# Rotations, score sums and convolution taps of a token mixer: running values in PSUM banks instead of SBUF tiles

## The chip, the cores and the metric

One core of a Trainium2 chip runs the whole program in one launch. The metric is the device time of that launch in microseconds (us); the kernel before takes 1549.39 us as the median of three runs (1548.85 to 1549.53). Engines carry the names of the profile: PE is TensorE (matmuls), PEld its weight loads, DVE is VectorE, ACT is ScalarE, POOL is GpSimd, SP the sync engine, which issues most loads.

## The reference

Two layers of a decoder trunk over 512 tokens of width 1024, all in float32. Each layer is a token mixer, a residual LayerNorm, a feed-forward block with a short convolution and a second residual LayerNorm. The mixer is the part that the change touches:

```python
z = h @ w_in + b_in
u_pool, u_conv, q, k, v, qi, ki, wi, gates = split_cols(z, IN_SIZES)
q, k = rope(q), rope(k)                       # 8 query heads, 2 key heads of 64
qi, ki = rope(qi) * 64**-0.5, rope(ki)        # indexer: 8 heads of 64, one key
y_pool = pool_mixer(u_pool) @ w_pool_out      # windows 2, 4, 8, 16
y_conv = conformer_conv(u_conv) @ w_conv_out  # GLU, causal conv of 31 taps, LayerNorm, swish
score = sum_h wi[h] * relu(qi[h] . ki)        # causal
y_attn = attention over the 128 best keys of each query @ w_attn_out
h = layer_norm(alpha * h + (sum_i sigmoid(gate_i) * y_i) @ w_o)
```

`rope(x)` is `x * cos + swap_halves(x) * sin` with signs in the sine table.

## The kernel before

Activations stand transposed, channels on partitions and the 512 tokens along the free axis. Matrix products keep float32 accuracy by splitting each operand into a high and a low part and summing three products, so every weight chunk of 128x1024 is loaded by SP, rounded by ACT (L74, `w_hi`) and subtracted by DVE (L78, `w_lo`; some chunks on POOL, in two halves). There are 123 chunks per layer, 246 in all; `Weights.take` hands them out in the order in which they are used, and four pairs of split tiles are in flight.

The eight PSUM banks are dealt out by tag: three `a`, two `s`, two `p`, one `v` (`BANKS`). A tile of a tag waits for a bank of that tag whose last reader is done. Before the change a projection's bank is read by ACT into an SBUF tile (`t`, with the bias) and is free again.

`mix` runs once per layer. It starts with the projections of the indexer's key (`head.os[0]`), the attention's key (`head.os[1]`) and the first pooling tile, which the preceding block has prepared (`Head`). Then come the four tiles of the indexer's queries (two heads each), the pooling, gate and value tiles of the convolution, v, and the four tiles of the attention's queries. `rotate` turns a tile: four DMAs on ACT's queue swap the halves into a second tile (`sw`), POOL multiplies that by the sine table (L409), DVE multiplies the tile by the cosine table (L408) and adds the two (L410). `stack` rounds a rotated tile on ACT (L417) and subtracts on DVE (`split_lo`, L112).

Three kinds of work are generators, and the main line steps them between projections. `index_gen(i)`, for query blocks 1 to 3, computes for each of eight heads a product (bank `s`), a relu on ACT into a tile `u` (three of them), and a multiply-add on DVE into `sc`, the block's score (L475 for the first head, L477 for the others); it then finds the 128 best keys by 16 pairs of L484 and L485 and turns the score into a mask. `conv_gen` runs the 31 taps of the two halves of the convolution's channels: for each half seven taps on DVE (L592, L595), 23 by a scaling on ACT (L589, tile `cvt`, two of them) and an addition on POOL (L590), and the sum of both at L598. `attn_gen(i)` is the attention of a block. After q come eight gates of the pooling branch: a projection, a small projection `y`, and DVE's L729, which multiplies them and frees the bank of `y`; then further gates, the branch merge (L748, L762, L766) and the output projection.

The order on each engine isn't that of the code. The tile framework plans it from a timeline of its own and writes a fixed list per engine; each engine takes its list from front to back and waits at the first instruction whose inputs aren't there.

Of the kernel before, what the change touches and what calls it, by code (L numbers as in the profile page):

```python
# [11 lines left out]
AF = mybir.ActivationFunctionType  # L12
ALU = mybir.AluOpType
PSUM = bass.MemoryType.PSUM

P = 128
D = 1024
L = 512
# [71 lines left out]
def trunk_kernel(ctx, tc, x, positions, w, poolw, params, lnv, cons, out):  # L90
# [264 lines left out]
    def mix(l, head, prev, ln, nxt):  # L355
        es = ExitStack()
        with es:
# [8 lines left out]
            def t_slot(dt=F32):  # L366
                return slot("t", 4, dt)
# [33 lines left out]
            def rotate(t, c0, slot_a, slot_s):  # L401
# [5 lines left out]
                a = slot_a()  # L407
                V.tensor_tensor(out=a[:, 0:n], in0=t[:, 0:n], in1=cosT[:, c0:L], op=ALU.mult)  # L408
                G.tensor_tensor(out=sw[:, 0:n], in0=sw[:, 0:n], in1=sinT[:, c0:L], op=ALU.mult)  # L409
                V.tensor_tensor(out=a[:, 0:n], in0=a[:, 0:n], in1=sw[:, 0:n], op=ALU.add)  # L410
                return a[:, 0:n]
# [16 lines left out]
            a = rotate(t, 0, p_slot, p_slot)  # L428
# [10 lines left out]
            t = t_slot()  # L439
            A.activation(t, head.os[1], AF.Identity, bias=pb(1))  # L440
            a = rotate(t, 0, p_slot, p_slot)
# [11 lines left out]
            for j in range(4):  # L453
                o = in_tile(P)
                t = t_slot()
                A.activation(t[:, 0:L - P], o[:, 0:L - P], AF.Identity, bias=pb(2 + j))
                tag = "qa" if j < 2 else "qb"
                qi.append(stack(rotate(t, P, p_slot, p_slot), q_slot(tag)[:, 0:L - P], q_slot(tag)[:, 0:L - P]))
# [3 lines left out]
            def index_gen(i):  # L462
                wd = (i + 1) * P
                sc = slot(f"mask{i}", 1, F32, [P, wd])
                for hh in range(NH):
# [8 lines left out]
                    if hh == 0:  # L474
                        V.tensor_scalar(sc, rl[:, 0:wd], wc, None, op0=ALU.mult)  # L475
                    else:
                        V.scalar_tensor_tensor(out=sc, in0=rl[:, 0:wd], scalar=wc, in1=sc,  # L477
                                               op0=ALU.mult, op1=ALU.add)
# [95 lines left out]
            def conv_gen():  # L574
                accs = []
                for c in range(2):
                    acc, pacc = c_slot()[:, 0:L], c_slot()[:, 0:L]
# [20 lines left out]
                    V.tensor_tensor(out=acc, in0=acc, in1=pacc, op=ALU.add)  # L598
                    accs.append(acc)
# [59 lines left out]
            for j in range(4):  # L659
                o = in_tile()  # L660
                t = t_slot()
                A.activation(t, o, AF.Identity, bias=pb(13 + j))
                stack(rotate(t, 0, t_slot, t_slot), qa_hi[:, j, :], qa_lo[:, j, :])
                step(1.5, 8)
# [252 lines left out]
```

## Time and profile before

| what | value |
|---|---|
| median of three runs | 1549.39 us (1548.85 to 1549.53) |
| profiled execution, its own time | 1548.56 us |
| its span, first to last instruction | 1546.8 us |
| mean granted TensorE clock | 0.983 of the upper level |
| PE busy | 1467.5 us, 95% of the span |
| DVE busy | 1007.5 us, 65% |
| ACT busy | 683.6 us, 44% |
| POOL busy | 538.1 us, 35% |

The shares are means over stages that are limited by different engines. The first mix begins at about 40 us and the second at about 798 us; the feed-forward blocks take up the rest. The table of stages gives each engine's busy time in a stretch, the granted clock and the DMA share; the list by form gives for each kind of instruction its count, busy time, mean duration in ns and the idle time in front of it.

### The profile page before, as it was taken

The numbers are of one execution on the slowest core, as the hardware profiler recorded it, in microseconds if no ns is written. First come the engines' busy times: TensorE is split into PE (matmuls) and PEld (weight loads), VectorE is DVE, ScalarE is ACT, GpSimd is POOL, SyncE is SP. The second block draws the span as 40 slices with busy tenths as digits, with TensorE's granted clock in tenths as the row PEclk, the third lists the DMA queues.
The fourth block names the chain that finished last, engine by engine and source line by source line (L and its number), as shares of the span: only waits on it lengthen the run. The fifth ranks groups of instructions, "written<-read, shape, count | busy, mean of one in ns | idle before, by whom it ended". The sixth has DMA issues, their size and how long they took to land.

```text
span 1546.8 us, 18617 instructions
## 1 busy us (share of the span) xinstructions
PE 1467.5 (95%) x6850; PEld 1218.1 (79%) x6850; DVE 1007.5 (65%) x1600; ACT 683.6 (44%) x1064; POOL 538.1 (35%) x395
## 2 busy tenths in 40 slices
PE   5998789999999999999999978999999999999997
PEld 5876678887888888888898756888878788888886
DVE  6799998756665555523268999976556655554234
ACT  5666636542444444421256664555326444443110
POOL 2357842209471111100134687231375511111004
PEclk9999999999999999999999989999999999999999
DMA  4422222223233333333234222222333333332331
GB/s 147 143 85 83 68 82 69 69 86 105 72 123 106 96 95 96 98 98 101 86 106 122 74 63 82 83 69 72 105 94 105 119 106 96 96 96 87 105 100 64
DMA packets 45019, 145.02 MB, mean 94 GB/s; under 512 B 6144, under 2 KB 7808, under 8 KB 44928
## 3 DMA queue, kind: packets, MB, share of 16 engines
q1 hardware_dynamic: 37632, 133.55, 28.1%
q10 hardware_dynamic: 7296, 10.29, 2.3%
q8 instruction: 54, 0.88, 0.2%
q14 instruction: 37, 0.30, 0.1%
HBM read 137.00 MB, written 2.10 MB: 90 GB/s over the span
## 4 chain that ended last, share of the span: by engine, by line
PE 70%; DVE 15%; POOL 7%; issue 4%; ACT 2%; DMA 2%; ACTq 0%; POOLq 0%; DVEq 0%
PE pb_a L289 15%; PE pb_a L290 15%; PE pb_a L291 15%; POOL h L221 3%; DVE w_lo L78 2%; POOL h L220 2%; PE pb_a L318 2%; PE pb_a L317 2%; PE pb_a L316 2%; DVE mask L477 2%; DVE mask L485 2%; PE pb_p L318 2%; PE pb_p L317 2%; PE pb_p L316 2%; PE pb_s L318 1%
## 5 line engine op out<-in xcount | busy, mean ns | idle before, releaser
L289 PE MATMUL pb_a<-hT_hi,w_hi 128*128 128x512 f32 (+1 forms) x1264 | 498.4, 394 | 35.8 <-DVE part L729 26.6
L78 DVE TENSOR_TENSOR w_lo<-w_raw,w_hi 128x1024 fp32r<-128x1024 f32 x210 | 290.3, 1383 | 339.9 <-ACT w_hi L74 338.9
L290 PE MATMUL pb_a<-hT_lo,w_hi 128*128 128x512 f32 (+1 forms) x1264 | 496.9, 393 | 0.0
L291 PE MATMUL pb_a<-hT_hi,w_lo 128*128 128x512 f32 (+1 forms) x1264 | 496.3, 393 | 0.0
L74 ACT ACTIVATE w_hi<-w_raw 128x1024 fp32r<-128x1024 f32 x246 | 260.6, 1059 | 400.0 <-PE pb_a L290 166.3
L289 PEld LDWEIGHTS pb_a<-hT_hi,w_hi 128*128 128x128 f32 x1264 | 241.2, 191 | 87.6 <-DVE part L729 29.9
L291 PEld LDWEIGHTS pb_a<-hT_hi,w_lo 128*128 128x128 f32 x1264 | 241.1, 191 | 47.4
L290 PEld LDWEIGHTS pb_a<-hT_lo,w_hi 128*128 128x128 f32 x1264 | 241.0, 191 | 46.5
L78 POOL TENSOR_TENSOR w_lo<-w_raw,w_hi 128x512 fp32r<-128x512 f32 x72 | 103.7, 1462 | 269.9 <-ACT w_hi L74 269.9
L800 POOL TENSOR_TENSOR fu<-fu 128x512 f32<-128x512 f32 x44 | 61.2, 1391 | 356.5 <-DVE fu L794 356.5
L590 POOL TENSOR_TENSOR cv<-cv,cvt 128x512 f32<-128x512 f32 x92 | 143.1, 1557 | 54.1 <-ACT cvt L589 46.5
L589 ACT ACTIVATE cvt<-cv,par 128x512 f32<-128x512 f32 x92 | 65.5, 721 | 28.0 <-POOL cv L590 27.7
L799 ACT ACTIVATE fu<-fu 128x512 f32<-128x512 f32 x44 | 27.8, 632 | 81.7 <-DVE fu L794 81.7
L794 DVE SCALAR_TENSOR_TENSOR fu<-pb_a,par,fu 128x510 f32<-128x510 f32 x82 | 61.4, 749 | 2.7
L791 ACT ACTIVATE fu<-pb_a,par 128x512 f32<-128x512 f32 x82 | 62.4, 761 | 0.0
L792 DVE SCALAR_TENSOR_TENSOR fu<-pb_a,par,fu 128x511 f32<-128x511 f32 x82 | 60.9, 743 | 0.0
L220 POOL TENSOR_TENSOR h<-h,gbt 128x512 f32<-128x512 f32 x32 | 52.1, 1660 | 18.3 <-DMA gbt<-in_lnv_dram 18.3
L683 ACT ACTIVATE qa<-qa,mx 128x128 f32<-128x128 f32 (+3 forms) x64 | 35.8, 560 | 51.1 <-DVE mx L680 48.2
L484 DVE MAX8 m<-mask 128x8 f32<-128x256 f32 (+2 forms) x96 | 52.8, 553 | 1.0
L208 ACT ACTIVATE gbt<-pb_a,par 128x128 f32<-128x128 f32 x96 | 35.7, 467 | 39.9 <-PE pb_a L200 39.9
L485 DVE MATCH_REPLACE8 mask<-m,mask 128x256 f32<-128x256 f32 (+2 forms) x96 | 51.9, 541 | 0.1
L316 PE MATMUL pb_a<-w_hi,g_hi 128*128 128x512 f32 x132 | 51.3, 389 | 0.0
(289 smaller groups left out, 2539.5 us busy)
## 6 DMA issues: line engine op xcount, KB each, us to landing
w_raw<-in_w_dram SPq DMA_DIRECT2D x246, 512.0 KB, 3.6
gbt<-in_lnv_dram ACTq DMA_DIRECT2D x20, 256.0 KB, 3.5
h<-in_x_dram SPq DMA_DIRECT2D x4, 512.0 KB, 5.5
t<-t ACTq DMA_DIRECT2D x32, 64.0 KB, 2.0
out_dram<-h SPq DMA_DIRECT2D x8, 256.0 KB, 2.0
part<-t ACTq DMA_DIRECT2D x32, 48.0 KB, 3.1
part<-t ACTq DMA_DIRECT2D x16, 64.0 KB, 4.1
par<-in_params_dram SPq DMA_DIRECT2D x2, 143.5 KB, 6.5
```

What stands on the lines that cost most here:

```text
L74: nc.scalar.activation(hi, raw, AF.Copy)
L78: eng.tensor_tensor(out=lo[:, cs], in0=raw[:, cs], in1=hi[:, cs].bitcast(F32), op=ALU.subtract)
L220: G.tensor_tensor(out=hb, in0=hb, in1=gb[0][c], op=ALU.mult)
L289: T.matmul(o, wh, xh(xc), start=(i == 0), stop=False)
L290: T.matmul(o, wh, xl(xc), start=False, stop=False)
L291: T.matmul(o, wl, xh(xc), start=False, stop=(i == n - 1))
L316: first = T.matmul(po[b], lh(k, b), wh, start=(k == 0), stop=False)
L318: T.matmul(po[b], ll(k, b), wh, start=False, stop=(k == nk - 1))
L485: V.match_replace(out=sc, in_to_replace=m8, in_values=sc, imm_value=FILL)
L589: A.activation(tm, hp[c][:, i:i + L], AF.Copy, scale=tap(i))
L590: G.tensor_tensor(out=pacc, in0=pacc, in1=tm, op=ALU.add)
L791: A.activation(t, o, AF.Identity, bias=par[:, l, PO_FB + ct:PO_FB + ct + 1], scale=tapw(2))
```

## The change

`rotate` now takes the projection's bank `o` itself. ACT still writes the biased SBUF tile `t`, from which the four DMAs swap halves, and POOL's product with the sine table is as before (`swapped`). DVE's first step adds the bias and multiplies by the cosine in one instruction in place in the bank, and its last step adds the swapped part in place in the bank. `stack` then reads the bank. The bank is held until the last split. The second and fourth tiles of both query groups take `p` banks instead of `a` banks. The indexer key's rotation stays in SBUF.

`index_gen` keeps the running score in the `v` bank; the last head's step writes the SBUF tile. `conv_gen` keeps DVE's running tap sum in a `p` bank, and the sum of both parts goes to the SBUF tile of POOL's part.

```diff
--- before.py
+++ after.py
@@ -398,17 +398,24 @@
             def drain(q):
                 pump(q, 1e9)
 
-            def rotate(t, c0, slot_a, slot_s):
+            def swapped(t, c0, slot_s):
                 n = L - c0
                 sw = slot_s()
                 for r in range(4):
                     nc.scalar.dma_start(out=sw[32 * r:32 * r + 32, 0:n],
                                         in_=t[32 * (r ^ 1):32 * (r ^ 1) + 32, 0:n])
-                a = slot_a()
-                V.tensor_tensor(out=a[:, 0:n], in0=t[:, 0:n], in1=cosT[:, c0:L], op=ALU.mult)
                 G.tensor_tensor(out=sw[:, 0:n], in0=sw[:, 0:n], in1=sinT[:, c0:L], op=ALU.mult)
-                V.tensor_tensor(out=a[:, 0:n], in0=a[:, 0:n], in1=sw[:, 0:n], op=ALU.add)
-                return a[:, 0:n]
+                return sw[:, 0:n]
+
+            def rotate(o, bias, c0, slot_s):
+                n = L - c0
+                t = t_slot()
+                A.activation(t[:, 0:n], o[:, 0:n], AF.Identity, bias=bias)
+                V.scalar_tensor_tensor(out=o[:, 0:n], in0=o[:, 0:n], scalar=bias, in1=cosT[:, c0:L],
+                                       op0=ALU.add, op1=ALU.mult)
+                sw = swapped(t, c0, slot_s)
+                V.tensor_tensor(out=o[:, 0:n], in0=o[:, 0:n], in1=sw, op=ALU.add)
+                return o[:, 0:n]
 
             UP, DN = slice(0, 64), slice(64, 128)
 
@@ -425,7 +432,9 @@
             A.activation(t[64:128], o[0:64], AF.Identity, bias=pb(0)[0:64])
             wis = t_slot()[0:8]
             A.activation(wis, o[64:72], AF.Identity, bias=pb(0)[64:72])
-            a = rotate(t, 0, p_slot, p_slot)
+            a = p_slot()[:, 0:L]
+            V.tensor_tensor(out=a, in0=t, in1=cosT, op=ALU.mult)
+            V.tensor_tensor(out=a, in0=a, in1=swapped(t, 0, p_slot), op=ALU.add)
             ki_hi, ki_lo = q_slot("qa"), q_slot("qa")
             A.activation(ki_hi, a, AF.Copy)
             split_lo(ki_lo, a, ki_hi)
@@ -436,9 +445,7 @@
             V.tensor_scalar(wq, wq_ps[:, 0:24], float(8 ** -0.5), 0.125, op0=ALU.mult, op1=ALU.mult)
 
             qi = []
-            t = t_slot()
-            A.activation(t, head.os[1], AF.Identity, bias=pb(1))
-            a = rotate(t, 0, p_slot, p_slot)
+            a = rotate(head.os[1], pb(1), 0, p_slot)
             kk_hi = q_slot("qc"), q_slot("qc")
             kk_lo = q_slot("qc"), q_slot("qc")
             for g, r in enumerate((UP, DN)):
@@ -451,17 +458,16 @@
             G.memset(up[0][:, 0:16], 0.0)
             A.activation(up[0][:, 16:], head.os[2], AF.Identity, bias=pb(6))
             for j in range(4):
-                o = in_tile(P)
-                t = t_slot()
-                A.activation(t[:, 0:L - P], o[:, 0:L - P], AF.Identity, bias=pb(2 + j))
+                o = in_tile(P, "a" if j % 2 == 0 else "p")
                 tag = "qa" if j < 2 else "qb"
-                qi.append(stack(rotate(t, P, p_slot, p_slot), q_slot(tag)[:, 0:L - P], q_slot(tag)[:, 0:L - P]))
+                qi.append(stack(rotate(o, pb(2 + j), P, p_slot), q_slot(tag)[:, 0:L - P], q_slot(tag)[:, 0:L - P]))
 
             masks = [tri] + [None] * 3
 
             def index_gen(i):
                 wd = (i + 1) * P
                 sc = slot(f"mask{i}", 1, F32, [P, wd])
+                acc = bank("v")[:, 0:wd]
                 for hh in range(NH):
                     j, r = hh // 2, hh % 2
                     qc = slice((i - 1) * P, i * P)
@@ -472,10 +478,10 @@
                     A.activation(rl[:, 0:wd], lg[:, 0:wd], AF.Relu)
                     wc = wq[:, (i - 1) * 8 + hh:(i - 1) * 8 + hh + 1]
                     if hh == 0:
-                        V.tensor_scalar(sc, rl[:, 0:wd], wc, None, op0=ALU.mult)
+                        V.tensor_scalar(acc, rl[:, 0:wd], wc, None, op0=ALU.mult)
                     else:
-                        V.scalar_tensor_tensor(out=sc, in0=rl[:, 0:wd], scalar=wc, in1=sc,
-                                               op0=ALU.mult, op1=ALU.add)
+                        V.scalar_tensor_tensor(out=acc if hh < NH - 1 else sc, in0=rl[:, 0:wd], scalar=wc,
+                                               in1=acc, op0=ALU.mult, op1=ALU.add)
                     yield wd * 0.00104 + 0.07
                 dg = sc[:, i * P:wd]
                 V.tensor_tensor(out=dg, in0=dg, in1=ctri, op=ALU.add)
@@ -574,7 +580,7 @@
             def conv_gen():
                 accs = []
                 for c in range(2):
-                    acc, pacc = c_slot()[:, 0:L], c_slot()[:, 0:L]
+                    acc, pacc = bank("p"), c_slot()[:, 0:L]
 
                     def tap(i):
                         k = PO_CW + c * CW + i
@@ -595,8 +601,8 @@
                             V.scalar_tensor_tensor(out=acc, in0=hp[c][:, i:i + L], scalar=tap(i),
                                                    in1=acc, op0=ALU.mult, op1=ALU.add)
                         yield 1
-                    V.tensor_tensor(out=acc, in0=acc, in1=pacc, op=ALU.add)
-                    accs.append(acc)
+                    V.tensor_tensor(out=pacc, in0=acc, in1=pacc, op=ALU.add)
+                    accs.append(pacc)
                     yield 1
                 xn = []
                 for bp in range(2):
@@ -657,10 +663,8 @@
             qa_lo = slot("qa_lo", 1, F32R, [P, 4, L])
             qa = (qa_hi, qa_lo)
             for j in range(4):
-                o = in_tile()
-                t = t_slot()
-                A.activation(t, o, AF.Identity, bias=pb(13 + j))
-                stack(rotate(t, 0, t_slot, t_slot), qa_hi[:, j, :], qa_lo[:, j, :])
+                o = in_tile(0, "a" if j % 2 == 0 else "p")
+                stack(rotate(o, pb(13 + j), 0, t_slot), qa_hi[:, j, :], qa_lo[:, j, :])
                 step(1.5, 8)
```

The order on DVE, ACT, PE and POOL moves inside both mixes; SP's order is the same. Three places, all in the first mix:

POOL during the convolution (`cv` are its accumulators, `cvt` the scaled taps, `t` with `sinT` the sine products of the four q tiles, `ln_rs` the convolution's LayerNorm). Before, then changed:

```order
L590 TENSOR_TENSOR cv<-cv,cvt 128x512 x10
L409 TENSOR_TENSOR t<-t,sinT 128x512
L590 TENSOR_TENSOR cv<-cv,cvt 128x512 x4
L409 TENSOR_TENSOR t<-t,sinT 128x512
L590 TENSOR_TENSOR cv<-cv,cvt 128x512 x4
L409 TENSOR_TENSOR t<-t,sinT 128x512
L590 TENSOR_TENSOR cv<-cv,cvt 128x512 x3
L409 TENSOR_TENSOR t<-t,sinT 128x512
L590 TENSOR_TENSOR cv<-cv,cvt 128x512 x14
L78 TENSOR_TENSOR w_lo<-w_raw,w_hi 128x512 x2
L590 TENSOR_TENSOR cv<-cv,cvt 128x512 x4
L78 TENSOR_TENSOR w_lo<-w_raw,w_hi 128x512 x2
```

```order
L596 TENSOR_TENSOR cv<-cv,cvt 128x512 x10
L407 TENSOR_TENSOR t<-t,sinT 128x512
L596 TENSOR_TENSOR cv<-cv,cvt 128x512 x12
L407 TENSOR_TENSOR t<-t,sinT 128x512
L596 TENSOR_TENSOR cv<-cv,cvt 128x512 x2
L407 TENSOR_TENSOR t<-t,sinT 128x512
L596 TENSOR_TENSOR cv<-cv,cvt 128x512 x8
L407 TENSOR_TENSOR t<-t,sinT 128x512
L596 TENSOR_TENSOR cv<-cv,cvt 128x512 x14
L78 TENSOR_TENSOR w_lo<-w_raw,w_hi 128x512 x4
L625 TENSOR_TENSOR ln_rs<-ln_ve,mhalf 128x1 x4
```

The products of the second and third q tile moved behind more additions, and the weight splits behind all of them.

DVE where the second q tile's last rotation step stands (before: `t_1257`; changed: `pb_p_1221`; `mask1` and `mask2` are score blocks in selection, `pb_v` the third block's running score, L598 and L604 the first half's tap sum). Before, then changed:

```order
L484 MAX m8_976<-mask1_748 128x8
L78 TENSOR_TENSOR w_lo_1441<-w_raw_1438,w_hi_1440 128x1024
L410 TENSOR_TENSOR t_1257<-t_1257,t_1252 128x512
L485 MATCH_REPLACE mask1_748<-m8_976,mask1_748 128x256
L477 SCALAR_TENSOR_TENSOR mask2_1034<-u_1192,wq_482,mask2_1034 128x384
L408 TENSOR_TENSOR t_1329<-t_1322,cosT_104 128x512
L484 MAX m8_979<-mask1_748 128x8
L481 TENSOR_TENSOR mask2_1034<-mask2_1034,ctri_97 128x128
L112 TENSOR_TENSOR qa_hi_1129<-t_1257,qa_hi_1129 64x512
L112 TENSOR_TENSOR qa_lo_1130<-t_1257,qa_lo_1130 64x512
```

```order
L491 MATCH_REPLACE mask1_743<-m8_1020,mask1_743 128x256
L483 SCALAR_TENSOR_TENSOR pb_v_1622<-u_1638,wq_482,pb_v_1622 128x512
L417 TENSOR_TENSOR pb_p_1221<-pb_p_1221,t_1249 128x512
L490 MAX m8_1023<-mask1_743 128x8
L483 SCALAR_TENSOR_TENSOR pb_v_1622<-u_1702,wq_482,pb_v_1622 128x512
L604 TENSOR_TENSOR cv_1104<-pb_p_1103,cv_1104 128x512
L491 MATCH_REPLACE mask1_743<-m8_1023,mask1_743 128x256
L483 SCALAR_TENSOR_TENSOR pb_v_1622<-u_1708,wq_482,pb_v_1622 128x512
L112 TENSOR_TENSOR qa_hi_1126<-pb_p_1221,qa_hi_1126 64x512
```

In the changed list the add stands among the score steps of the third block, and the first half's tap sum follows three rows behind it; the splits follow the add as before.

PE where the projection of the fourth q tile begins (before: `pb_a_1372`; changed: `pb_p_1366`; `pb_s` are head scores). Before, then changed:

```order
L469 MATMUL pb_s_1183<-qa_474,qb_708 128x384
L470 MATMUL pb_s_1183<-qa_475,qb_708 128x384
L290 MATMUL pb_a_1297<-hT_lo_103,w_hi_1133 128x512
L291 MATMUL pb_a_1297<-hT_hi_102,w_lo_1134 128x512
L289 MATMUL pb_a_1372<-hT_hi_102,w_hi_1221 128x512
L290 MATMUL pb_a_1372<-hT_lo_103,w_hi_1221 128x512
L291 MATMUL pb_a_1372<-hT_hi_102,w_lo_1222 128x512
```

```order
L475 MATMUL pb_s_1705<-qa_474,qb_656 128x512
L476 MATMUL pb_s_1705<-qa_475,qb_656 128x512
L475 MATMUL pb_s_1711<-qa_474,qb_657 128x512
L476 MATMUL pb_s_1711<-qa_475,qb_657 128x512
L475 MATMUL pb_s_1717<-qa_474,qb_703 128x512
L476 MATMUL pb_s_1717<-qa_475,qb_703 128x512
L289 MATMUL pb_p_1366<-hT_hi_102,w_hi_1217 128x512
L290 MATMUL pb_p_1366<-hT_lo_103,w_hi_1217 128x512
L291 MATMUL pb_p_1366<-hT_hi_102,w_lo_1218 128x512
```

The projection moved behind head scores of the third score block, and into a `p` bank.

## Rows read from the trace of the kernel before

**Rows 1.** Table of stages: stretch, length, busy time (count) of PE, PEld, DVE, ACT, POOL, clock, DMA

```profile
45.00:60.00 15.00, 15.00 (x87) 14.56 (x86) 10.02 (x14) 8.35 (x12) 4.04 (x3) 1.00 0.60 164
60.00:210.00 150.00, 127.94 (x528) 102.14 (x527) 147.03 (x221) 86.61 (x136) 103.02 (x68) 0.92 0.28 85
210.00:350.00 140.00, 140.00 (x675) 115.16 (x675) 102.91 (x249) 72.71 (x139) 31.35 (x26) 1.00 0.26 78
...
825.00:970.00 145.00, 122.87 (x513) 98.39 (x512) 141.38 (x219) 82.33 (x131) 101.01 (x65) 0.93 0.27 79
970.00:1110.00 140.00, 140.00 (x672) 115.10 (x671) 102.01 (x245) 72.37 (x139) 33.70 (x27) 1.00 0.26 80
```

**Rows 2.** The page, busy time, share of the span and count of each engine

```profile
PE 1467.5 (95%) x6850; PEld 1218.1 (79%) x6850; DVE 1007.5 (65%) x1600; ACT 683.6 (44%) x1064; POOL 538.1 (35%) x395
```

**Rows 3.** Waits of PE from 45 to 260 us, and PE in time order

```profile
PE pb_a L289 <- DVE part L729: 13.3, 5, 5.7
...
203.13 0.80 PE L289 MATMUL pb_a<-hT_hi,w_hi 128*128 128x512 f32 x1 [4.98 <-DVE part L729]
...
961.06 0.79 PE L289 MATMUL pb_a<-hT_hi,w_hi 128*128 128x512 f32 x1 [4.97 <-DVE part L729]
```

**Rows 4.** DVE, then POOL, in time order: start, duration, line, in the first mix

```profile
173.33 1.23 DVE L595 SCALAR_TENSOR_TENSOR cv<-cv,par 128x512 f32<-128x512 f32 x1
174.48 0.68 DVE L729 SCALAR_TENSOR_TENSOR part<-t,pb_a 128x512 f32<-128x512 f32 x1
175.08 1.16 DVE L477 SCALAR_TENSOR_TENSOR mask<-u,wq,mask 128x512 f32<-128x512 f32 x1
...
178.40 0.74 DVE L595 SCALAR_TENSOR_TENSOR cv<-cv,par 128x512 f32<-128x512 f32 x1
...
172.06 3.63 POOL L78 TENSOR_TENSOR w_lo<-w_raw,w_hi 128x512 fp32r<-128x512 f32 x2 [0.27 <-ACT w_hi L74]
175.65 1.74 POOL L590 TENSOR_TENSOR cv<-cv,cvt 128x512 f32<-128x512 f32 x1
179.32 4.04 POOL L590 TENSOR_TENSOR cv<-cv,cvt 128x512 f32<-128x512 f32 x3 [1.92 <-ACT cvt L589]
```

**Rows 5.** Groups of DVE instructions by form: count, busy us, mean ns, idle before

```profile
L595 DVE SCALAR_TENSOR_TENSOR cv<-cv,par 128x512 f32<-128x512 f32 x24 | 31.0, 1291 | 0.3
...
L477 DVE SCALAR_TENSOR_TENSOR mask<-u,wq,mask 128x512 f32<-128x512 f32 x14 | 17.6, 1256 | 0.0
...
L477 DVE SCALAR_TENSOR_TENSOR mask<-u,wq,mask 128x384 f32<-128x384 f32 x14 | 13.2, 940 | 0.0
...
L477 DVE SCALAR_TENSOR_TENSOR mask<-u,wq,mask 128x256 f32<-128x256 f32 x14 | 9.0, 646 | 0.4
...
L410 DVE TENSOR_TENSOR t<-t 128x512 f32<-128x512 f32 x8 | 9.5, 1186 | 0.0
...
L410 DVE TENSOR_TENSOR part<-part 128x384 f32<-128x384 f32 x8 | 8.1, 1016 | 0.1
...
L408 DVE TENSOR_TENSOR part<-t,cosT 128x384 f32<-128x384 f32 x8 | 8.5, 1065 | 0.2
...
L112 DVE TENSOR_TENSOR qa_lo<-t,qa_lo 64x512 fp32r<-64x512 f32 x8 | 12.1, 1514 | 0.2
...
L112 DVE TENSOR_TENSOR qa_hi<-t,qa_hi 64x512 fp32r<-64x512 f32 x8 | 8.5, 1066 | 0.2
...
L112 DVE TENSOR_TENSOR qb<-part,qb 64x384 fp32r<-64x384 f32 x8 | 7.3, 917 | 0.8 <-ACT qb L417 0.6
...
L729 DVE SCALAR_TENSOR_TENSOR part<-t,pb_a 128x512 f32<-128x512 f32 x16 | 10.7, 670 | 0.0
...
L680 DVE CUSTOM_DVE_ANT_0 qa<-pb_s,mask 128x384 f32<-128x384 f32 x16 | 8.6, 550 | 3.3 <-PE pb_p L693 3.3
...
L792 DVE SCALAR_TENSOR_TENSOR fu<-pb_a,par,fu 128x511 f32<-128x511 f32 x82 | 60.9, 743 | 0.0
```

**Rows 6.** POOL's tap additions: over the run, in the first mix, and in time order

```profile
L590 POOL TENSOR_TENSOR cv<-cv,cvt 128x512 f32<-128x512 f32 x92 | 143.1, 1557 | 54.1 <-ACT cvt L589 46.5 <-DMA t<-t 2.8
...
L590 POOL TENSOR_TENSOR cv<-cv,cvt x46: 1267/1588/2266, 91.8 to 196.6; 128x512 f32<-128x512 f32 x46
...
147.90 6.93 POOL L590 TENSOR_TENSOR cv<-cv,cvt 128x512 f32<-128x512 f32 x4
```

## The prediction

> **What bounds the kernel now.** I read the table of stages first. Each of the two mixes has a stretch in which VectorE is busy almost without a gap and TensorE is not: 147.03 of 150 us in the first, 141.38 of 145 in the second, with TensorE at 127.94 and 122.87 and a granted clock of 0.92 and 0.93 of its upper level [rows 1]. In the 140 us behind each of them TensorE is busy all the time and VectorE is not. Over the whole span VectorE is busy for only 65% [rows 2], so the average hides where it rules.
>
> Then the waits of TensorE in the first stretch: the largest is on L729, VectorE's product that frees the bank of a branch output, 13.3 us in 5 waits; the last one ends at 203.13 us in the first mix and at 961.06 in the second, each with 5.0 us of idle time [rows 3]. After these TensorE runs full. So what VectorE saves in front of that instruction is saved for the end, as long as TensorE has idle time to give: 22.1 us in each stretch, and some more from matmuls at the lower clock.
>
> Next, why VectorE is so full. In one piece of time order the same kind of instruction has two lengths [rows 4]. The convolution tap L595 takes 1.23 us at 173.33, while GpSimd works on L78, and 0.74 us at 178.40, when GpSimd is idle (from 177.39 to 179.32). The score sum L477 at 175.08 takes 1.16. Both read two SBUF tiles. L729 at 174.48 takes 0.68 while GpSimd is busy: it has one operand in PSUM. Over the whole run it holds: L729 has a mean of 670 ns, the kinds of 384 and 512 columns with two SBUF tiles 917 to 1514 ns [rows 5]. So VectorE and GpSimd hold each other up when both work on SBUF tiles, and a PSUM operand takes VectorE out of it.
>
> **The change, part by part.** Per mix 78 VectorE instructions get one operand in PSUM: 9 first and 9 last steps of rotations, 20 low-part splits, 24 score steps, 14 taps and 2 tap sums. None is added. For the new durations I take the nearest PSUM rows: 670 ns for 512 columns (L729), 550 for 384 (L680), 743 where a per-partition scalar is read too (L792), hence 623 at 384 and, by the same step, about 495 at 256 columns [rows 5]. The savings, both mixes:
>
> Score sums L477: 14 x (1256-743) + 14 x (940-623) + 14 x (646-495) = 13.7 us. Taps L595: 24 x (1291-743) = 13.2. Last rotation step L410: 8 x (1186-670) + 8 x (1016-550) = 7.9. Splits of qa_lo, qa_hi and qb: 8 x (1514-670) + 8 x (1066-670) + 8 x (917-550) = 12.9. First rotation step at 384 columns: 8 x (1065-623) = 3.5. The rest (L598, L592, L475, the other splits and first steps) I estimate at 5.5; some of these lose, as the first tap and first score step are short when nothing disturbs them. Together 57 us, 28 per mix [rows 5].
>
> Not all of that lies in front of the release that TensorE waits for, because VectorE's order changes as well. I added the durations row by row in VectorE's order, from the first weight split behind the rotation tables (second mix: from the first rotation step) to the sixth bank release: before, 159.5 us in the first mix and 158.1 in the second; changed, 147.1 and 140.3. The difference is 12.4 and 17.8 us. The other 16 and 10 us go to work now done earlier: rows of the first attention block, the convolution's statistics, and selection steps of the last score block. TensorE is full when these used to run, so nothing comes back for them. To check the sum: it puts the release 43.6 us in front of where TensorE resumes (203.13 - 159.5), and VectorE starts that list at about 41 and idles some 3 us.
>
> From these 12.4 and 17.8 I take waits that become visible. Early in the mix TensorE is the limit already (15.00 of 15 us from 45 to 60, VectorE 10.02 [rows 1]), so the first rotations and scores can't come much earlier: 2 us per mix. Then GpSimd. The product with the sine table for the second q tile stands behind 22 convolution additions and one other product in GpSimd's order (before: behind 14 and one). VectorE arrives at the add that needs it 83.5 us into its list, at 43.6 + 83.5 = 127.1 us. The first addition starts at 91.8 us now [rows 6] and, with its gate product some 4 us earlier, at about 88. 24 instructions at the shortest duration, 1267 ns, end at 118; at the mean of 1557 at 125 [rows 5, 6]; at the present pace with all its gaps, 2.33 us each (27 instructions from 91.8 to 154.8 [rows 6]), at 144. GpSimd is held up less too, so I take a pace near 1.7, an end at 129, a wait of 2 and 1 more for the adds behind it: 3 us per mix. What is queued behind VectorE's add is selection, the tap sum and the splits that free the bank.
>
> The bank is the third new wait. One of the two p banks holds the running tap sum, so v, the second and the fourth q tile pass through the other, and TensorE meets the fourth tile's projection in its fixed order, with the gates behind it. It has to wait for the second tile's last split. That split lies 6 us behind the add in VectorE's list, TensorE has one small projection and five head scores to fill it, and the wait falls where TensorE has idle time anyway. I price it at 0, with GpSimd's wait as its limit.
>
> ScalarE's copies read PSUM instead of SBUF: bounded by its own idle time, 0. The rotations keep their four DMA each and drop one SBUF tile: 0. The sync queue's order is the same: 0.
>
> Sum: 12.4 + 17.8 - 2 x (2 + 3) = **20 us** less than the profiled execution's 1548.56, 1528.5. That execution lies 0.8 below the median of 1549.39, so I say **1529**.
>
> No VectorE instruction in this trace writes PSUM, and 53 of the 78 will. Nearest rows: 670 ns (reads PSUM, writes SBUF) from below, and above the 1256 to 1291 ns that the same kinds take now [rows 5]. I take the PSUM-read rows, since reading shows no extra time at all; the upper end would leave only the splits' gain, about 6 us per mix, which the waits eat.
>
> A rule speaks against the change: the Trainium skill, "Perfetto Trace Analysis", Optimizing Scalar/DVE Operations, gives a VectorE instruction about 60 ns of access overhead on SBUF and about 125 on PSUM. By it 78 instructions would cost an estimated 5 us per mix, and the result would be near 1539. The rows for reads don't show that: L729 at 670 ns is shorter than an undisturbed tap at 0.74 us [rows 4, 5].
>
> **The rivals.** (a) *GpSimd paces the mix.* Its weight split for the sixth gate stood among the additions and started at 172.06 [rows 4]; now it stands behind all 46. From 88 us, 46 additions, 4 products and the 2 split halves at 1.7 us end at 176, in time, as TensorE begins that gate at about 176. But from 91.8 to the end of the last addition, 198.2 by its start of 196.6 and the mean duration, the present pace is about 2.0 with gaps [rows 5, 6]; then it ends at 192, TensorE reaches the eighth gate's wait at about 205 against 203.13, and nothing is gained: about **1549**. For it: GpSimd's gaps come from ScalarE, which hasn't less to do. Against: a good part of ScalarE's waits are on VectorE.
>
> (b) *Slower: the add that stands behind 22 additions.* If GpSimd keeps 2.33 us per instruction, VectorE waits until 144 instead of 127, 16 us per mix with the splits, the bank and TensorE's gates behind it. Then -12.4 + 2 + 16 = +5.6 and -17.8 + 2 + 16 = +0.2: about **1555**. It decides from a wait of 13 us on, (30.2 - 4) / 2, a pace of 2.2 us. Against it: the pace of 2.33 holds 4 products and gaps behind VectorE's slow rotations, which the change removes.
>
> (c) *A PSUM write costs more than a read.* With 70 ns more, the step between 670 and 743, 53 writes cost 3.7 us per mix: about **1536**. Nothing in the trace speaks for or against; the rule quoted above would give a similar result.
>
> (d) *It doesn't do what it says*, as VectorE's long instructions are long for another reason. Speaks against it: the undisturbed 0.74 at 178.40 [rows 4]. I give it no share of its own.
>
> **How the numbers follow.** My forecast, 1512 to 1540, gets 0.62; (a) 0.14, (b) 0.13, (c) 0.06; 0.05 is for what I don't see, both ways. A difference under 0.2%, 3 us, can't be told from none. Faster: 0.62 + 0.06 + 0.05 of (a) + 0.02 = 0.75. Same: 0.08 of (a) and 0.02 of (b) = 0.10. Slower: 0.15. The range reaches down to the full 30 us and some 8 more where GpSimd finishes early and leaves the remaining splits alone, 1511, and up to 1553, which takes in (a) and the lower half of (b).
>
> **What would show it.** Right: score steps, taps and rotation steps at 0.62 to 0.75 us; GpSimd's additions nearer to 1.35 us than 1.56; TensorE's last wait on a branch product some 8 us earlier in its mix in the first, 13 in the second, and 12 us less idle time before it. Wrong: idle time of VectorE above some 8 us per mix, ended by GpSimd's sine product (b); TensorE waiting on a weight split from GpSimd (a); PSUM-writing instructions above 0.8 us (c).

## The result and the profile after

The changed kernel took 1521.36 us (median of 4 runs, 1520.71 to 1524.27) against 1549.29 for the kernel before (4 runs). The ratio is 0.9828, 95% interval 0.9816 to 0.9840: 28 us, 1.7%, faster. The forecast was 1529 in a range from 1511 to 1553. Profiled execution against profiled execution it is 1524.27 against 1548.56 us, 24.3 less: the profiled execution is the slowest of the four, so some 3 of the 28 us don't show in the trace.

The stages of the changed kernel, in the table of stages (busy time and count of PE, PEld, DVE, ACT and POOL, clock, DMA share, GB/s), with the same first stretches as [rows 1]; the second mix begins some 12 us earlier here:

```profile
45.00:60.00 15.00, 15.00 (x87) 14.62 (x87) 10.40 (x13) 7.94 (x11) 4.04 (x3) 1.00 0.68 203
60.00:210.00 150.00, 135.78 (x591) 109.70 (x590) 137.60 (x283) 94.64 (x153) 93.14 (x73) 0.94 0.28 82
210.00:350.00 140.00, 140.00 (x666) 115.50 (x665) 91.30 (x198) 66.37 (x127) 39.05 (x30) 1.00 0.28 91
820.00:960.00 140.00, 131.18 (x566) 106.05 (x565) 128.16 (x262) 87.77 (x137) 88.75 (x66) 0.94 0.28 83
960.00:1100.00 140.00, 139.84 (x660) 114.28 (x659) 90.08 (x199) 64.92 (x128) 41.73 (x30) 1.00 0.26 85
```

From 60 to 210 us TensorE is busy 7.8 us more than before and VectorE 9.4 us less. The page's busy times, against [rows 2]:

```profile
PE 1461.4 (96%) x6850; PEld 1214.9 (80%) x6850; DVE 949.2 (62%) x1600; ACT 680.5 (45%) x1064; POOL 509.4 (33%) x395
```

VectorE lost 58.3 us (forecast 57) and GpSimd 28.7. TensorE's idle time, span less busy time, fell from 79.3 to 60.8 us, and its busy time by 6.1 us, at a granted clock of 0.987 and not 0.983 over the span. The groups by form (count, busy us, mean ns, idle before) answer to [rows 5]; L483 is L477 of before, L601 L595, L417 L410, L414 L408, L598 the first tap (before L592):

```profile
L601 DVE SCALAR_TENSOR_TENSOR pb_p<-cv,par,pb_p 128x512 f32<-128x512 f32 x24 | 17.9, 745 | 0.1
...
L483 DVE SCALAR_TENSOR_TENSOR pb_v<-u,wq,pb_v 128x512 f32<-128x512 f32 x12 | 8.9, 742 | 0.0
...
L483 DVE SCALAR_TENSOR_TENSOR pb_v<-u,wq,pb_v 128x384 f32<-128x384 f32 x12 | 7.3, 608 | 0.0
...
L483 DVE SCALAR_TENSOR_TENSOR pb_v<-u,wq,pb_v 128x256 f32<-128x256 f32 x12 | 5.8, 483 | 1.3 <-ACT u L478 1.2
...
L598 DVE TENSOR_SCALAR pb_p<-cv,par 128x512 f32<-128x512 f32 x4 | 3.0, 742 | 0.0
...
L112 DVE TENSOR_TENSOR qa_lo<-pb_a,qa_lo 64x512 fp32r<-64x512 f32 x4 | 2.8, 693 | 0.1
...
L417 DVE TENSOR_TENSOR pb_p<-pb_p,t 128x512 f32<-128x512 f32 x4 | 2.8, 691 | 2.3 <-POOL t L407 2.3
L417 DVE TENSOR_TENSOR pb_a<-pb_a,t 128x512 f32<-128x512 f32 x4 | 2.7, 684 | 0.0
```

The same groups of GpSimd, against [rows 6]:

```profile
L596 POOL TENSOR_TENSOR cv<-cv,cvt 128x512 f32<-128x512 f32 x92 | 131.5, 1430 | 48.8 <-ACT cvt L595 44.3
```

And what TensorE waits for in the first mix (45 to 260 us), against [rows 3]; L733 is L729 of before:

```profile
PE pb_s L475 <- ACT u L478: 5.6, 3, 5.1
PE pb_p L289 <- DVE cv L604: 2.3, 1, 2.3
PE pb_a L289 <- ACT t L719: 2.3, 1, 2.3
PE pb_s L680 <- DVE mx L684: 1.4, 1, 1.4
PE pb_a L289 <- DVE qa L112: 1.1, 1, 1.1
PE pb_a L289 <- DVE part L733: 1.0, 1, 1.0
PE pb_a L291 <- DVE w_lo L78: 0.4, 1, 0.4
```

The wait on the branch products has gone from 13.3 to 1.0 us. What is left lies earlier, in the q tiles: on the scores' ReLU tiles, and on L604, the tap sum of the convolution's first half, which the fourth q tile waits for because the sum sits in a p bank.

### The profile page after: what moved, and what is told of

Its sections match the earlier page's. It is cut to its first block, busy times and chain, and to the rows that moved or that the text cites. A ratio compares the mean times of both kernels' runs of the same rounds, so it can differ in the third digit from the quotient of the medians.

```text
span 1522.2 us, 18587 instructions
## 1 busy us (share of the span) xinstructions
PE 1461.4 (96%) x6850; PEld 1214.9 (80%) x6850; DVE 949.2 (62%) x1600; ACT 680.5 (45%) x1064; POOL 509.4 (33%) x395
## 4 chain that ended last, share of the span: by engine, by line
PE 75%; POOL 8%; DVE 7%; DMA 3%; issue 3%; ACT 3%; ACTq 0%; POOLq 0%; DVEq 0%
PE pb_a L289 16%; PE pb_a L291 16%; PE pb_a L290 16%; POOL h L221 3%; POOL h L220 3%; PE pb_a L318 2%; PE pb_a L317 2%; PE pb_a L316 2%; PE pb_p L318 2%; PE pb_p L317 2%; PE pb_p L316 2%; PE pb_s L318 2%; PE pb_s L316 1%; PE pb_s L317 1%; POOL part L767 1%
## 5 line engine op out<-in xcount | busy, mean ns | idle before, releaser
L78 DVE TENSOR_TENSOR w_lo<-w_raw,w_hi 128x1024 fp32r<-128x1024 f32 x210 | 285.0, 1358 | 374.9 <-ACT w_hi L74 374.2
L289 PE MATMUL pb_a<-hT_hi,w_hi 128*128 128x512 f32 (+1 forms) x1200 | 471.1, 393 | 9.6 <-ACT t L719 4.2
L291 PE MATMUL pb_a<-hT_hi,w_lo 128*128 128x512 f32 (+1 forms) x1200 | 469.6, 391 | 1.8 <-DVE w_lo L78 1.8
L290 PE MATMUL pb_a<-hT_lo,w_hi 128*128 128x512 f32 (+1 forms) x1200 | 469.4, 391 | 0.0
L289 PEld LDWEIGHTS pb_a<-hT_hi,w_hi 128*128 128x128 f32 x1200 | 226.9, 189 | 56.5 <-ACT t L719 5.1
L291 PEld LDWEIGHTS pb_a<-hT_hi,w_lo 128*128 128x128 f32 x1200 | 226.7, 189 | 48.3 <-DVE w_lo L78 2.4
L290 PEld LDWEIGHTS pb_a<-hT_lo,w_hi 128*128 128x128 f32 x1200 | 227.0, 189 | 44.6
L78 POOL TENSOR_TENSOR w_lo<-w_raw,w_hi 128x512 fp32r<-128x512 f32 x72 | 97.4, 1376 | 300.3 <-ACT w_hi L74 291.6
L596 POOL TENSOR_TENSOR cv<-cv,cvt 128x512 f32<-128x512 f32 x92 | 131.5, 1430 | 48.8 <-ACT cvt L595 44.3
L595 ACT ACTIVATE cvt<-cv,par 128x512 f32<-128x512 f32 x92 | 64.8, 719 | 25.0 <-POOL cv L596 24.0
```

What stands on the lines that cost most here:

```text
L78: eng.tensor_tensor(out=lo[:, cs], in0=raw[:, cs], in1=hi[:, cs].bitcast(F32), op=ALU.subtract)
L289: T.matmul(o, wh, xh(xc), start=(i == 0), stop=False)
L290: T.matmul(o, wh, xl(xc), start=False, stop=False)
L291: T.matmul(o, wl, xh(xc), start=False, stop=(i == n - 1))
L595: A.activation(tm, hp[c][:, i:i + L], AF.Copy, scale=tap(i))
L596: G.tensor_tensor(out=pacc, in0=pacc, in1=tm, op=ALU.add)
```

## The experiments

The diff has three things that can be separated: the sums of scores and taps in PSUM (S), the rotations in PSUM (R), and the alternation of the eight rotated tiles between a and p banks (A). All eight combinations were run, then three refinements and one kernel with GpSimd's additions left out. Medians of the kernel before were 1548.5 to 1549.6 in all comparisons.

**One part at a time.** e1 is the change's part in `index_gen`, e2 that in `conv_gen`, e3 the rest, R and A; e4 takes A out of the changed kernel:

```diff
-                o = in_tile(P, "a" if j % 2 == 0 else "p")
+                o = in_tile(P)
...
-                o = in_tile(0, "a" if j % 2 == 0 else "p")
+                o = in_tile()
```

> The kernel before with only the running sum of the index scores in a PSUM bank. Theory (each part is worth the VectorE time it saves ahead of the late releases): the 24 score instructions of a mix fall from 940-1256 ns to about 745, 608 and 483 ns, 6.9 us less VectorE per mix, 3 to 3.5 us less at TensorE's end per mix, time near 1543 us. Rival (only the rotations matter, since they free SBUF tiles and hold banks otherwise): score instructions as short as that, but a time within 2 us of the kernel before.

> The kernel before with only VectorE's convolution taps summed in a PSUM bank. Theory: the 12 taps that also read the sum fall from 1291 to about 745 ns, 6.6 us less VectorE per mix, time near 1543 us; GpSimd's additions (1557 ns) get shorter by some 50 ns, as the two meet less often. Rival (only the rotations matter): within 2 us of the kernel before. Second rival (GpSimd paces the convolution): within 2 us too, with GpSimd's additions ending when they did.

> The kernel before with only the rotations in PSUM (index q tiles and q tiles, with every second one of them in a p bank). Theory: some 30 of the 57 us of VectorE time, so about half of the 28 us: near 1535 us, and the three parts add up to about 28. Rival (only the rotations matter): near 1522 us, with nothing left for the other two.

> The changed kernel with all eight rotated tiles of a mix in the three a banks again, none in a p bank; the rest as changed. Theory that the prediction took (the alternation costs and gives about nothing): within 3 us of the changed kernel's 1521 us. Rival (a rotated tile now holds its bank until the last split, some 5 us longer than the tile that ScalarE used to copy out, so the alternation is what makes the change pay): TensorE waits for a banks at the index q tiles and the q tiles, 2 to 5 us more per mix, near 1528 us. Other rival (the p bank delays the convolution's banks behind it, the 2.3 us wait of TensorE on the fourth index tile's bank): faster than the changed kernel by 2 to 5 us.

Measured: 1539.46 (e1), 1537.27 (e2), 1537.44 (e3) and 1532.46 us (e4). Each part is worth 10 to 12 us, more than VectorE's time ahead of the release gave for the first two and a little less than the 14 of e3's theory. The rivals of e1, e2 and e3 fall. GpSimd's additions got 31 ns shorter in e2 (1557 to 1525) where 50 were expected. e4's rival with the banks held too long is right and too small: without the alternation the changed kernel loses 11 us, although VectorE's busy time is the same (949.0). The scores depend on where the taps are. With the taps alone in PSUM, the scores of 384 columns, left in SBUF, got longer, 940 ns before and 1312 in e2:

```profile
L477 DVE SCALAR_TENSOR_TENSOR mask<-u,wq,mask 128x384 f32<-128x384 f32 x14 | 18.4, 1312 | 0.1
```

**The other combinations.** f1 is A alone, f2 is S, f3 S and A, f4 R alone with all tiles in a banks. f1:

```diff
-                o = in_tile(P)
+                o = in_tile(P, "a" if j % 2 == 0 else "p")
...
-                o = in_tile()
+                o = in_tile(0, "a" if j % 2 == 0 else "p")
```

> The kernel before with nothing in PSUM that was not there; only the banks of the eight rotated tiles alternate between a and p. Theory 1 (the alternation spares TensorE waits for a banks in any kernel): 8 to 11 us faster than before, 1538 to 1541 us. Theory 2 (it pays only where a rotated tile keeps its bank through the rotation): before copies the tile out at once, so within 2 us of 1549 us.

> The kernel before with the scores' and the taps' running sums in PSUM, rotations in SBUF, no alternation. If the parts add up: 9.9 + 12.1 us, 1527 us. If both saved the same wait of TensorE: no better than either, 1536 us. If it is under 1532 us, rotations in PSUM with all tiles in a banks make the kernel slower, since the changed kernel without the alternation took 1532 us.

> Scores and taps in PSUM, rotations in SBUF, and the alternation of banks. It has all of the change but the rotations. Theory 1 (the alternation pays by itself): below 1520 us, as good as the changed kernel or better with some 16 us more VectorE time in a mix. Theory 2 (the alternation pays only with the rotations): equal to scores and taps without it, near 1527 us.

> The kernel before with only the rotations in PSUM, all tiles in a banks. The run with the alternation took 1537 us. Theory of the prediction (VectorE time counts, some 30 us of it over both mixes): 1537 us too. Rival (a rotated tile now holds its a bank until the last split, so TensorE waits for a bank earlier): 1545 to 1555 us, with waits of TensorE for a banks in the index and the q tiles.

Measured, with VectorE's busy time of the profiled execution beside the median, in us:

| in the kernel | all tiles in a banks | alternating a and p |
|---|---|---|
| none of it | before: 1549.4, VectorE 1007.5 | f1: 1559.2, VectorE 1014.1 |
| R | f4: 1549.5, VectorE 977.4 | e3: 1537.4, VectorE 982.3 |
| S | f2: 1518.5, VectorE 980.4 | f3: 1528.1, VectorE 970.2 |
| S and R | e4: 1532.5, VectorE 949.0 | changed kernel: 1521.4, VectorE 949.2 |

Both theories on the alternation fall, in f1 and in f3: by itself it costs 10 us, with or without S, and where the rotations are in PSUM it saves 11 to 12. S alone saves 31 us, more than either forecast of f2 and more than the whole change: 3 us better than the changed kernel (ratio to before 0.9795, 0.9782 to 0.9808) with 31 us more of VectorE time. Alone, its halves gave 9.9 and 12.1; together they give 9 more. The likely reason is that neither is left in SBUF beside GpSimd: VectorE's busy time falls by 11.3 and 10.6 us alone and by 27.1 together. R takes 30 us from VectorE in f4 and saves nothing, as its rival has it, ratio 1.0000 (0.9991 to 1.0009). f4's stages from 45 us on show where that went:

```profile
45.00:75.00 30.00, 22.11 (x107) 20.33 (x106) 19.71 (x28) 14.08 (x23) 9.77 (x9) 0.83 0.50 142
75.00:105.00 30.00, 30.00 (x140) 25.02 (x139) 21.64 (x24) 16.10 (x25) 12.65 (x10) 1.00 0.24 77
105.00:135.00 30.00, 22.53 (x98) 17.84 (x97) 29.60 (x59) 21.53 (x36) 18.72 (x13) 0.96 0.31 90
135.00:165.00 30.00, 25.64 (x96) 19.76 (x94) 29.46 (x50) 21.25 (x33) 24.00 (x17) 0.87 0.24 69
```

Before, TensorE was busy 28.12, 29.73, 27.40 and 19.80 us in these four. f4 gains 5.8 in the last (and 3.5 from 165 to 210 us, 41.39 against 37.89) and loses 6.0 in the first and 4.9 in the third. Its longest waits of TensorE from 20 to 260 us point to the cause, the rotated tiles' splits:

```profile
PE pb_a L289 <- DVE qa_lo L112: 9.3, 3, 4.4
PE pb_s L474 <- DVE qa L112: 7.1, 1, 7.1
```

Before, ScalarE copied a tile out and its bank was free; TensorE went through the index tiles without a wait (15.00 of 15 us from 45 to 60 us, [rows 1]). Now an index tile that ScalarE reads at 50.90 us keeps its bank through the rotation; with three a banks the fourth index tile starts at 63.17, as the rows of f4 in time order show (PE's first row is a score that the order puts ahead of that tile):

```profile
50.90 0.58 ACT L413 ACTIVATE t<-pb_a,par 128x384 f32<-128x384 f32 x1
```
```profile
61.61 0.55 PE L474 MATMUL pb_s<-qa 128*128 128x256 f32 x1 [7.09 <-DVE qa L112]
...
63.17 0.69 PE L289 MATMUL pb_a<-hT_hi,w_hi 128*128 128x384 f32 x1 [0.80 <-DVE qa L112]
```

The alternation gives the tiles a fourth and a fifth bank. In f1, where no tile needs them, the cost stands alone, as TensorE waits for the tap sum with the transposes of the convolution:

```profile
PE pb_p L607 <- DVE cv L598: 10.6, 2, 10.0
```

L598 starts at 154.0 us in f1 and at 153.7 before, where nobody waits for it. So it is not late. Before, TensorE comes to these transposes at 173.01 us; in f1 it has run out of other work in its fixed order at 144.7 and stands in front of them.

**Index tiles and q tiles apart, and the contention by itself.** g1 has S and, for the index tiles alone, R and A; its four q tiles are rotated in SBUF as before. g2 is the changed kernel with the q tiles, still in PSUM, in a banks (the second half of e4's diff). e5 is the kernel before with this line taken out:

```diff
                             A.activation(tm, hp[c][:, i:i + L], AF.Copy, scale=tap(i))
-                            G.tensor_tensor(out=pacc, in0=pacc, in1=tm, op=ALU.add)
```

> The changed kernel with the four q tiles' rotations as before (copied out at once to SBUF, all in a banks); scores, taps and the index rotations, these with alternating banks, stay in PSUM. The changed kernel took 1521 us, scores and taps alone 1518 us. Theory (the q tiles in PSUM cost TensorE time between 105 and 165 us, where it is busy 47.9 of 60 us against 53.3 with scores and taps alone, since their banks are held to the last split and two of them are p banks that the convolution wants): TensorE busy over 52 us of those 60, time 1510 to 1517 us, the best so far. Rival (the index tiles are what costs): at or above 1521 us.

> The changed kernel with the four q tiles in the three a banks, still rotated in PSUM; the index tiles as changed, alternating a and p. With all eight tiles in a banks it took 1532 us, with all alternating 1521 us. If the alternation pays at the index tiles (TensorE busy 22.3 of the 30 us from 45 on without it, 28.9 with it): 28 to 29 us there, time 1521 us or below; below 1518 us if the p bank is what costs the q tiles. If it pays at the q tiles: near 1532 us, with waits for a banks between 105 and 165 us.

> The kernel before, all in SBUF, with GpSimd's 44 tap additions of a mix left out: ScalarE still makes the products, nobody adds them. Theory (VectorE's instructions with two SBUF operands are long because GpSimd works at the same time): the taps of 1291 ns fall below 900 ns, the scores of 1256 ns too, with no bank in play; TensorE's waits on the branch products shrink and the time falls by 15 to 30 us, as with scores and taps in PSUM. Rival (these instructions are long for their operands, whoever else works): taps stay above 1150 ns.

Measured: 1516.01 (g1), **1509.40** (g2, ratio to before 0.9747, 0.9734 to 0.9760) and 1498.29 us (e5; the additions are 46 in a mix [rows 6], 44 was a miscount).

g2 beats both kernels, by 39 and by 12 us, and its stage from 45 to 75 us has TensorE busy for 28.73 us, as expected if the alternation pays at the index tiles. The alternation is worth 23 us at the index tiles (e4 to g2) and costs 12 at the q tiles (g2 to the changed kernel). g1 came out as its theory forecast, at 1516 us with TensorE busy for 52.04 of the 60 us. But in a banks the rotation of the q tiles in PSUM does pay, 6.6 us from g1 to g2, so the theory, that holding the banks costs there, is half wrong: it is their being p banks. VectorE's instructions on p banks from 100 to 175 us (x count: shortest/median/longest ns, first and last start) show what comes with it, first in the changed kernel, then in g2:

```profile
L601 DVE SCALAR_TENSOR_TENSOR pb_p<-cv,par,pb_p x12: 734/744/755, 111.0 to 161.5; 128x512 f32<-128x512 f32 x12
...
L598 DVE TENSOR_SCALAR pb_p<-cv,par x2: 737/740/742, 110.0 to 145.2; 128x512 f32<-128x512 f32 x2
```
```profile
L601 DVE SCALAR_TENSOR_TENSOR pb_p<-cv,par,pb_p x12: 734/742/752, 110.7 to 141.9; 128x512 f32<-128x512 f32 x12
...
L598 DVE TENSOR_SCALAR pb_p<-cv,par x2: 740/744/748, 109.7 to 118.6; 128x512 f32<-128x512 f32 x2
```

With two q tiles passing through p, the first tap of the convolution's second half starts at 145.2 us and not 118.6, and the last tap 20 us later. In the changed kernel TensorE's wait for the first half's sum, in front of the fourth q tile, ends at 137.73 us; g2 has no such wait. The stage from 105 to 165 us, in the changed kernel and in g2:

```profile
105.00:165.00 60.00, 47.95 (x189) 37.20 (x188) 58.16 (x123) 41.97 (x72) 46.09 (x35) 0.86 0.22 61
```
```profile
105.00:165.00 60.00, 53.36 (x223) 41.78 (x222) 59.37 (x115) 44.51 (x74) 50.11 (x36) 0.91 0.26 74
```

TensorE is busy 5.4 us more in g2, at a higher mean clock, with 34 more matmuls. That sharing banks with the tap sum makes the 12 us is read from these rows and not tried by itself. TensorE's new order is the rival: in f1, where no tap sum sits in a p bank, the alternation cost 10 us too, and in the changed kernel the longest wait of this stage, 5.1 us, is on a ReLU tile of the head scores that the order puts in front of the fourth q tile.

e5 shows the contention without any bank. VectorE's long instructions, all in SBUF, at the lengths they have when GpSimd doesn't add:

```profile
L594 DVE SCALAR_TENSOR_TENSOR cv<-cv,par 128x512 f32<-128x512 f32 x24 | 18.0, 749 | 0.3
...
L477 DVE SCALAR_TENSOR_TENSOR mask<-u,wq,mask 128x512 f32<-128x512 f32 x14 | 10.3, 737 | 0.0
L477 DVE SCALAR_TENSOR_TENSOR mask<-u,wq,mask 128x384 f32<-128x384 f32 x14 | 8.5, 610 | 0.1
...
L410 DVE TENSOR_TENSOR t<-t 128x512 f32<-128x512 f32 x8 | 5.5, 686 | 5.9 <-POOL t L409 5.9
...
L591 DVE TENSOR_SCALAR cv<-cv,par 128x512 f32<-128x512 f32 x4 | 1.9, 482 | 0.1
```

1291 ns became 749, 1256 became 737, 1186 became 686: the operands don't make them long, GpSimd does. The rotations of 384 columns run early in the mix, beside GpSimd's other work, and stay long on average in e5 (L410 1026 ns, before 1016); the shortest of them takes 553:

```profile
L410 DVE TENSOR_TENSOR part<-part x12: 553/692/1421, 48.6 to 808.3; 128x384 f32<-128x384 f32 x8, 128x512 f32<-128x512 f32 x4
```

The time fell by 50 us, more than the 15 to 30 expected. The likely reason is that the end of GpSimd's chain is gone as well; that was not tried by itself.

**Fewer taps on VectorE.** h2 starts from g2:

```diff
-                        if i % 4 != 0:
+                        if i % 6 != 0:
```

> The best version so far (index rotations alternating a and p, q tiles rotated in a banks; 1509 us) with every sixth tap on VectorE in place of every fourth: 5 of 30 in each half and not 7, so 4 taps of 0.74 us less on VectorE in a mix and 4 additions of 1.43 us more on GpSimd. Theory (VectorE still sets the pace between 105 and 165 us; GpSimd, which adds until 178 us, is waited for by nobody): TensorE's idle time there falls by up to 3 us a mix, time 1503 to 1508 us. Rival (GpSimd paces the convolution now): its additions end some 6 us later and TensorE waits for the convolution's products or for weights that GpSimd splits, 1512 to 1520 us.

Measured: 1509.34 us, the same as g2; neither theory. GpSimd's additions end later, with their last start at 183.2 us and not 177.8, and TensorE waits 0.6 us in the first mix on the tap sum that needs them. But VectorE got nothing back: the 8 taps less are 5.9 us, and its busy time is 950.1 against 947.8 us. So 8.2 us came in elsewhere, and 4.4 of them are the softmax scaling L690, on SBUF tiles: 34.3 us and not 29.9. It meets GpSimd more: laid over GpSimd's rows, 16 of its 64 instructions in g2 and 20 in h2 run while GpSimd works, at a mean of 729 and 886 ns, and the others take 394 and 393.

## Why the prediction was right, and the step that was wrong

*What bounds the kernel.* Right. TensorE's waits on the branch products were the largest, and they went (13.3 to 1.0 us in the first mix).

*Why VectorE was full, and the new durations.* Right, and shown by e5. The sum of 57 us came out at 58.3. Taken 743, 623 and 495 for the scores, measured 742, 608 and 483; splits 670 taken, 684 to 693 measured.

*PSUM writes* (rival c). Refuted: 684 to 691 ns for L417, which writes PSUM, beside 686 in e5 for the same step undisturbed on SBUF. By the overheads that the Trainium skill, "Perfetto Trace Analysis", Optimizing Scalar/DVE Operations, gives for VectorE (about 60 ns on SBUF, about 125 on PSUM) it would be an estimated 65 ns longer on PSUM; no two-operand row here shows that. One kind does lose by a PSUM write: the first tap, with one tensor operand, takes 742 ns into PSUM (L598) and 482 undisturbed on SBUF (L591 in e5). Beside GpSimd it took 1021 before, so here it gains all the same. The Trainium skill, "VectorE: DVE Perf Modes", Why PSUM operands drop a tier, says that a PSUM operand excludes the doubled rate for such instructions in fp32. It argues from the reading side; here the bank is only written, and the two rows agree with it.

*The releases.* Nearly right. In the changed kernel the sixth release starts at 194.91 us in the first mix and 937.06 in the second:

```profile
194.91 0.67 DVE L733 SCALAR_TENSOR_TENSOR part<-t,pb_a 128x512 f32<-128x512 f32 x1
...
937.06 0.65 DVE L733 SCALAR_TENSOR_TENSOR part<-t,pb_a 128x512 f32<-128x512 f32 x1
```

Before it was at 202.40 and 960.33. The first is 7.5 us earlier, forecast 7.4; the second 11.2 beyond what the first mix had gained at its end, forecast 12.8. That is luck in part, as two sizes are wrong and cancel. VectorE's stretch up to the release, before and in the changed kernel, first mix (the third busy time and count are VectorE's):

```profile
40.00:203.08 163.08, 141.07 (x629) 116.26 (x627) 153.33 (x218) 98.83 (x151) 107.06 (x71) 0.94 0.31 92
```
```profile
40.00:195.58 155.58, 141.36 (x645) 117.43 (x644) 136.42 (x265) 99.95 (x157) 92.73 (x72) 0.95 0.33 96
```

Its busy time there fell by 16.9 us, and by 19.6 in the second mix, where 12.4 and 17.8 were taken from durations added row by row; neighbouring rows overlap a little, so such a sum runs above the busy time, and the "some 3 us" of idle time that checked it are 8.7 in the trace. The waits of VectorE grew by 9.1 and 8.0 us, where 5 were deducted. Of the "3 us per mix" for GpSimd's sine product VectorE waited 1.0 us in the first mix and 1.3 in the second for that of the q tile, so rival (b) is refuted. In place of the "2 us per mix" of TensorE's early limit, VectorE waited 7.5 us more than before in the first mix and 7.7 in the second for ScalarE's halves of the weights (L78, 4.3 to 11.8 us from 40 to 165 us).

*"Nothing comes back for them"*, for the 16 and 10 us of work that is done earlier. More did come behind the releases, and this is what made the forecast 4 us too small on the profiled executions. TensorE's first matmul behind the first mix (L200) came at 391.97 and 1136.44 us, and before at 404.00 and 1161.84:

```profile
391.97 0.71 PE L200 MATMUL pb_a<-ident,h 128*128 128x128 f32 x5
...
1136.44 0.82 PE L200 MATMUL pb_a<-ident,h 128*128 128x128 f32 x6
```

So the mixes gave 12.0 and 13.4 us, 4.5 and 2.1 more than the releases; 0.8 of it is lost behind the second mix (the spans differ by 24.6). Most of this is TensorE's clock, which the sum gave no term: the prediction speaks of "some more from matmuls at the lower clock" and leaves it there. Before, TensorE has been idle for 5.0 us when the sixth release comes, and its granted clock is then at the lower level (0.50, 1.2 GHz) for the next 12 matmuls in each mix:

```profile
203.13:208.40 5.27, 5.27 (x12) 4.13 (x13) 5.20 (x15) 0.12 (x1) 0.00 (x0) 0.50 0.33 130
961.06:966.20 5.14, 5.14 (x12) 4.08 (x13) 5.07 (x15) 0.00 (x0) 0.00 (x0) 0.50 0.39 136
```

They start 0.43 us apart, and the same matmuls 0.23 apart once the clock is back at its upper level, so the clock costs an estimated 2.5 us a mix there. In the changed kernel TensorE doesn't stop in front of the release, and the clock stays at the upper level. The stretch from the release to L200 of the first mix, before and changed:

```profile
203.13:403.80 200.67, 198.68 (x910) 160.88 (x910) 140.18 (x302) 85.58 (x156) 73.06 (x53) 0.99 0.27 85
```
```profile
195.60:391.70 196.10, 193.79 (x897) 157.85 (x896) 128.21 (x255) 82.94 (x150) 72.97 (x52) 1.00 0.27 87
```

So the clock accounts for all of the second mix's 2.1 us and over half of the first's 4.5. The other 2 us of the first go with the 13 matmuls fewer behind the release: part of what VectorE did earlier let TensorE do its share earlier too, in time that it had idle. For this part "nothing comes back" is wrong.

*The p bank, "priced at 0".* Wrong, and hidden by the total. TensorE did wait there for 2.3 us a mix, though on the tap sum and not on the second tile's last split. But the wait is the smaller part. With the q tiles in p banks the convolution's second half starts 27 us later, and the kernel takes 12 us more than g2; how much of that is the bank and how much TensorE's order stays open. The a banks stood in no sentence: with the q tiles in a banks, the alternation at the index tiles is worth 23 us (e4 to g2).

*What each part is worth.* The prediction counted all VectorE time ahead of a release alike. By the runs the 27 us from scores and taps are worth 31 us by themselves: in f2 TensorE's waits from 45 to 260 us add up to 10.1 us, before to 22.0, and none of them is on a rotated tile's split. The next 31 us, from the rotations, are worth 14 us less than nothing in e4, 3 less than nothing in the changed kernel and 8 to 9 more in g2, with VectorE's time the same within 1.4 us in all three. Had the banks been priced, the sum could have told these apart.

*Rival (a)*, GpSimd as the pace, is refuted: its additions end at about 177.5 us (198 before), and h2, where they end some 5 us later than in g2, takes no longer. *Rival (d)* is refuted by e5.

## What to carry to other kernels

In this kernel a VectorE operand moved to PSUM pays where VectorE and GpSimd hold each other up, and most for long-lived sums in banks that no projection is waiting for; move all the instructions that meet GpSimd together, since those left in SBUF can get longer, as the scores did in e2. Where the moved tile is the bank that TensorE writes next, price how long the bank is now held against how many there are, tile by tile. The same alternation of banks saved 23 us at one place of this kernel and cost 12 at another, so try each place by itself. And where a wait of TensorE goes away, look at its granted clock behind the wait as well: here that gave some 2.5 us a mix which the sum had left out.

## What was not expected of the hardware

The stretching can move instead of ending. With the taps alone in PSUM the scores of 384 columns went from 940 to 1312 ns (the taps, left in SBUF in e1, stayed at 1276), and with 8 taps fewer on VectorE, and 8 additions more on GpSimd, the softmax scaling got 4.4 us longer in total. GpSimd's own instructions differ as well between e5 and before: its weight split L78 has a mean of 1361 ns without its additions and 1462 with them.

What stays open: that TensorE's order in f1 meets the convolution's transposes 10 us early was read from the trace, but why it does was not tried, nor what part of the 12 us at the q tiles is the shared bank, nor whether a wider choice of banks at the q tiles (s, or a fourth a) would gain more than g2.
